# A hybrid decoder layer on one core: the input projections of both FFNs as seven block products

## The chip, the core and the metric

The kernel runs on one core of a Trainium2 chip. The core has TensorE (PE in the rows; its weight loads are PEld), VectorE (DVE), ScalarE (ACT), GpSimd (POOL) and SyncE (SP), which only issues transfers here. The metric is the device time of one execution in microseconds (us), and less is better.

## The reference, cut to what matters

One decoder layer on 512 tokens of width 1024, in float32: a half-step FFN, a token mixer, a second half-step FFN of the same shape, and a per-layer embedding. The change concerns the two FFNs:

```python
D_MODEL = 1024; SEQ = 512; D_FF = 2816

def swiglu(u, w_in, w_out):
    gate, up = jnp.split(u @ w_in, 2, axis=-1)
    return (jax.nn.silu(gate) * up) @ w_out

# step 1 and step 3 of the layer
h = h + 0.5 * rmsnorm(swiglu(rmsnorm(h, norm_pre), w_in, w_out), norm_post)
```

`u @ w_in` is the input projection: 512 tokens x 1024 by 1024 x 5632. `@ w_out` is the output projection, 2816 to 1024.

## The kernel before, in words

**Precision.** Every float32 matrix is held as two fp32r tiles, a rounded one (hi: `whi`, `uhi`) and the rest (lo: `wlo`, `ulo`). `mm3` makes one product of three matmuls: hi by hi, hi by lo, lo by hi (lines 100 to 102). ACT makes the hi tile by a cast, DVE the lo tile by a subtraction of two SBUF tiles: for a weight tile, line 91 is the cast and line 92 the subtraction.

**Input projection.** The 2816 hidden features are 22 tiles of 128, and a tile f has two weight chunks of 128 x 1024 (512 KB), gate and up. `wchunk` loads a chunk into one of two `raw` buffers over SP's queue and splits it into one of three `whi`/`wlo` pairs. In `ffn`, PE multiplies a chunk with all 512 tokens into one PSUM bank `pgu`: 8 parts of the 1024-deep sum by three matmuls of 512 columns, so 48 matmuls for a tile f. `ev` then takes the bank: ACT's Silu of the gate (line 259), DVE's product with the up part (262), and the split of the result into `hid[f]` (263 on ACT, 266 on DVE).

**Start of an FFN.** `make_u` normalises one tile of 128 tokens, PE transposes it into `put`, and ACT and DVE split it into `uhi` and `ulo`. Since tokens 0 to 255 come first, `start_tiles` runs the first chunks (6 in the first FFN, 4 in the second) in two halves of 256 columns; their bank is called `p` in the rows.

**After it.** `out_proj` multiplies `hid` with the output weights (bank `acc`), and norms and adds the result. Between the FFNs lies the mixer. Its rows serve below as examples: there GpSimd adds two SBUF tiles of 128 x 512 (line 983) while DVE splits weight tiles.

Each engine works through its instructions in one fixed order, which a scheduler chose from the program's order; an instruction that waits holds up all those behind it on its engine.

Of the kernel before, what the change touches and what calls it, by code (L numbers as in the profile page):

```python
# [32 lines left out]
def layer_kernel(ctx, tc, x, pT, wf1, wo1, wfm, wsm, wtm, wbr, wout, wf2, wo2, wgate, wproj,  # L33
# [82 lines left out]
    def u_at(u, k, n):  # L116
        return u[0][:, k, n], u[1][:, k, n]
# [10 lines left out]
    def first_u(tt, h, u, t):

        hs = sp.tile([128, 1], F32, name="hs", bufs=4)  # L130
        A.activation(t, h[:, tt, :], AF.Square, accum_out=hs)
        V.tensor_scalar(t, h[:, tt, :], inv_rms(hs, False), None, op0=ALU.mult)
        tk = slice(tt * 128, tt * 128 + 128)
        for j in range(2):
            pt = axp("put")
            for i in range(4):
                k = 4 * j + i
                tr(pt[:, i * 128:(i + 1) * 128], t[:, k * 128:(k + 1) * 128])
            for i in range(4):
                k = 4 * j + i  # L140
                g = cst[:, C_G + k:C_G + k + 1]
                pv = pt[:, i * 128:(i + 1) * 128]
                A.activation(u[0][:, k, tk], pv, AF.Copy, scale=g)
            for i in range(4):
                k = 4 * j + i
                g = cst[:, C_G + k:C_G + k + 1]
                pv = pt[:, i * 128:(i + 1) * 128]
                V.scalar_tensor_tensor(u[1][:, k, tk], pv, g, u[0][:, k, tk].bitcast(F32),
                                       op0=ALU.mult, op1=ALU.subtract)

    def make_u(tt, h, gn, u, t):
# [4 lines left out]
        V.scalar_tensor_tensor(t, h[:, tt, :], r, gn, op0=ALU.mult, op1=ALU.mult)  # L156
        tk = slice(tt * 128, tt * 128 + 128)
        for j in range(2):
            pt = axp("put")
            for i in range(4):  # L160
                k = 4 * j + i
                tr(pt[:, i * 128:(i + 1) * 128], t[:, k * 128:(k + 1) * 128])
            pv = pt.rearrange("p (a b) -> p a b", b=128)
            ks = slice(4 * j, 4 * j + 4)
            A.copy(u[0][:, ks, tk], pv)
            V.tensor_sub(u[1][:, ks, tk], pv, u[0][:, ks, tk].bitcast(F32))
# [53 lines left out]
                if ch:  # L220
                    close(tt, 1 + len(cut))

    def start_tiles(tiles, u):

        for si, n in enumerate(SEG):
            for i, (w, r, ev) in enumerate(tiles):
                ps = (mmp if si == 0 else axp)("p0")
                for k in range(KT):
                    mm3(ps[:r, n], cols(w, k * r, (k + 1) * r), u_at(u, k, n), k == 0, k == KT - 1)
                ev(n, ps)  # L230
# [7 lines left out]
    def start_weights(fp, wf, n, slots):  # L238
        for i in range(n):
            dst = None  # L240
            if i >= slots:
                c = 14 + 2 * (i - slots)
                dst = (fp.tile([128, 1024], F32R, name=f"xh{i}", tag=f"hid{c}"),
                       fp.tile([128, 1024], F32R, name=f"xl{i}", tag=f"hid{c + 1}"))
            yield wchunk(wf[i], dst=dst, eng=G if wf is wf2 and i > 1 else None)

    def ffn(fp, free, wf, wo, h, u, gi, gn_i, first):
        hid = [None] * FT
        marks = []
        g = {}  # L250

        def ev(f, part):
            def run(n, ps):
                if part == 0:
                    if f == 2 and len(first) == 6:
                        t = g[f] = lp.tile([128, T + 608], F32, name="gx")
                    else:
                        t = g[f] = sp.tile([128, T], F32, name="gt", tag="t512", bufs=2)
                    A.activation(t[:, n], ps[:, n], AF.Silu)
                else:  # L260
                    t = g[f]
                    V.tensor_tensor(t[:, n], ps[:, n], t[:, n], op=ALU.mult)  # L262
                    m = A.copy(hid[f][:, 0, n], t[:, n])
                    if f == 4:
                        marks.append(m)
                    V.tensor_sub(hid[f][:, 1, n], t[:, n], hid[f][:, 0, n].bitcast(F32))
            return run

        def hid_tile(f):
            return fp.tile([128, 2, T], F32R, name=f"hid{f}")  # L270

        nf = len(first) // 2
        for f in range(nf):
            hid[f] = hid_tile(f)
        start_tiles([(w, 128, ev(i // 2, i % 2)) for i, w in enumerate(first)], u)
        for f in range(nf, FT):
            hid[f] = hid_tile(f)
# [34 lines left out]
    with pool("s1", "right") as small:  # L312
        env.small = small
        f1_pool = ExitStack()
        fp = f1_pool.enter_context(pool("f1"))
        xt = [small.tile([128, D], F32, name=f"ys{i}") for i in range(2)]
# [5 lines left out]
        weights = start_weights(fp, wf1, 6, 2)  # L322
# [7 lines left out]
        u = new_u()  # L330
        for tt in range(4):
            if tt < 1:
                first_u(tt, h, u, xt[tt % 2])
            else:
                make_u(tt, h, gn, u, xt[tt % 2])
        u = ffn(fp, f1_pool.close, wf1, wo1, h, u, G_F1 + 1, G_MIX, first)
# [623 lines left out]
    if True:  # L960
# [27 lines left out]
        u2 = new_u()  # L988
# [132 lines left out]
```

## Time and profile before

| what | value |
|---|---|
| time, median of 3 runs | 1319.95 us (1317.66 to 1321.33) |
| time of the profiled execution | 1320.2 us |
| its span, first to last instruction | 1318.4 us |
| PE busy (98% of the span) | 1287.5 us |
| PEld busy | 1074.3 us |
| DVE busy | 639.3 us |
| ACT busy | 465.7 us |
| POOL busy | 70.0 us |
| bytes moved | 141.26 MB, 107 GB/s on average |

The profile is of one execution. The span is 1.8 us shorter than that execution's time. A matmul's busy time overlaps that of the next one, so the pace of PE is read from the distance of two starts, not from one duration. The first FFN's input projection lies at about 13 to 260 us of the span, the second one's at about 887 to 1130 us.

### The profile page before, as it was taken

To read this page: it belongs to the slowest core of one execution; us is meant where nothing else is said; L and a number is where in the kernel's file an instruction comes from. 1 tells how busy PE (TensorE), PEld (TensorE's weight loads), DVE (VectorE), ACT (ScalarE), POOL (GpSimd) and SP (SyncE) were. 2 spreads that over 40 slices of the span, in tenths; PEclk is the share of its full clock that TensorE was granted. 3 is DMA by queue.
4 is the path that set the end of the run, shared out by engine and by line. 5 is a ranking of instruction groups with operands and counts; after the bars stand their busy time and mean duration, and the time that the engine had idled before them with its cause. 6 is when DMAs were issued, how large, how long until landed. Compare 5 with 4: busy or idle time off the path is not lost.

```text
span 1318.4 us, 16647 instructions
## 1 busy us (share of the span) xinstructions
PE 1287.5 (98%) x6661; PEld 1074.3 (81%) x6661; DVE 639.3 (48%) x1088; ACT 465.7 (35%) x765; POOL 70.0 (5%) x71
## 2 busy tenths in 40 slices
PE   7999999999989999999999999989999999999997
PEld 6988888888879888877678888779888888888876
DVE  6233333323262699987686454463333333223465
ACT  6222222212253453454655222352222223112353
POOL 0000000000010000021002001220000000000000
PEclk9999999999999999999999999999999999999999
DMA  6243333223342223344206635522433333233431
GB/s 216 67 128 96 96 96 98 94 83 99 122 143 92 88 65 111 97 121 130 79 1 147 212 108 181 159 87 81 130 96 96 96 96 108 68 96 96 128 112 64
DMA packets 57772, 141.26 MB, mean 107 GB/s; under 512 B 17568, under 2 KB 20064, under 8 KB 57696
## 3 DMA queue, kind: packets, MB, share of 16 engines
q1 hardware_dynamic: 56688, 136.54, 33.9%
q10 hardware_dynamic: 1008, 3.67, 0.9%
q8 instruction: 52, 0.85, 0.3%
q14 instruction: 24, 0.20, 0.0%
HBM read 128.62 MB, written 11.57 MB: 106 GB/s over the span
## 4 chain that ended last, share of the span: by engine, by line
PE 86%; DMA 5%; DVE 5%; ACT 2%; issue 1%; POOL 0%; SPq 0%; DVEq 0%; POOLq 0%; ACTq 0%
PE pgu L101 11%; PE pgu L100 11%; PE pgu L102 11%; PE acc L101 5%; PE acc L102 5%; PE acc L100 5%; PE p L101 3%; PE p L100 3%; PE p L102 3%; PE ptm L101 2%; PE ptm L100 2%; PE ptm L102 2%; PE pg L100 2%; PE pg L102 2%; PE pg L101 2%; PE pat L713 2%
## 5 line engine op out<-in xcount | busy, mean ns | idle before, releaser
L91 ACT CAST whi<-raw 128x1024 fp32r<-128x1024 f32 x135 | 142.1, 1052 | 389.7 <-PE pgu L101 154.0
L92 DVE TENSOR_TENSOR wlo<-raw,whi 128x1024 fp32r<-128x1024 f32 x135 | 166.3, 1232 | 195.0 <-ACT whi L91 187.6
L100 PE MATMUL pgu<-uhi,whi 128*128 128x512 f32 x624 | 242.8, 389 | 0.0
L102 PE MATMUL pgu<-uhi,wlo 128*128 128x512 f32 x624 | 242.8, 389 | 0.0
L101 PE MATMUL pgu<-ulo,whi 128*128 128x512 f32 x624 | 242.7, 389 | 0.0
L100 PEld LDWEIGHTS pgu<-uhi,whi 128*128 128x128 f32 x624 | 117.1, 188 | 24.5
L102 PEld LDWEIGHTS pgu<-uhi,wlo 128*128 128x128 f32 x624 | 117.1, 188 | 24.4
L101 PEld LDWEIGHTS pgu<-ulo,whi 128*128 128x128 f32 x624 | 117.1, 188 | 24.0
L92 DVE TENSOR_TENSOR vlo<-raw,vhi 128x1024 fp32r<-128x1024 f32 x45 | 56.1, 1249 | 131.0 <-ACT vhi L91 130.9
L101 PE MATMUL acc<-vlo,hid 128*128 128x512 f32 x288 | 112.1, 389 | 0.0
L102 PE MATMUL acc<-vhi,hid 128*128 128x512 f32 x288 | 111.7, 389 | 0.0
L91 ACT CAST vhi<-raw 128x1024 fp32r<-128x1024 f32 x45 | 47.1, 1048 | 143.7 <-PE acc L102 123.3
L100 PE MATMUL acc<-vhi,hid 128*128 128x512 f32 x288 | 97.4, 389 | 0.0
L262 DVE TENSOR_TENSOR gt<-pgu,gt 128x512 f32<-128x512 f32 x39 | 27.0, 692 | 136.7 <-PE pgu L102 136.7
L78 POOL TENSOR_TENSOR rinv<-ms,mhalf 128x1 f32<-128x1 f32 x32 | 18.9, 594 | 844.0 <-DVE ms L123 844.0
L101 PEld LDWEIGHTS acc<-vlo,hid 128*128 128x128 f32 x288 | 54.1, 188 | 11.3
L100 PEld LDWEIGHTS acc<-vhi,hid 128*128 128x128 f32 x288 | 54.1, 188 | 11.2
L102 PEld LDWEIGHTS acc<-vhi,hid 128*128 128x128 f32 x288 | 54.0, 188 | 11.3
L101 PE MATMUL ptm<-wlo,uhi 128*128 128x512 f32 x128 | 50.3, 393 | 0.0
L100 PE MATMUL ptm<-whi,uhi 128*128 128x512 f32 x128 | 50.0, 395 | 0.0
L102 PE MATMUL ptm<-whi,ulo 128*128 128x512 f32 x128 | 49.8, 391 | 0.0
L100 PE MATMUL pg<-uhi,whi 128*128 128x512 f32 x104 | 41.2, 396 | 0.0
(394 smaller groups left out, 2335.9 us busy)
## 6 DMA issues: line engine op xcount, KB each, us to landing
raw<-wf SPq DMA_DIRECT2D x88, 512.0 KB, 3.6
raw<-wo SPq DMA_DIRECT2D x44, 512.0 KB, 3.6
raw<-wfm SPq DMA_DIRECT2D x28, 512.0 KB, 3.7
raw<-wtm SPq DMA_DIRECT2D x20, 512.0 KB, 3.7
gd<-gst SPq DMA_DIRECT2D x16, 256.0 KB, 2.1
raw<-wbr SPq DMA_DIRECT2D x8, 512.0 KB, 4.4
grl<-gd SPq DMA_DIRECT2D x16, 256.0 KB, 3.2
raw<-wout SPq DMA_DIRECT2D x8, 512.0 KB, 4.2
```

Source lines behind the costliest of these rows:

```text
L78: G.tensor_tensor(out_, in_, e, op=ALU.pow)
L91: A.copy(hi[:, :n], raw[:, :n])
L92: (eng or V).tensor_sub(lo[:, :n], raw[:, :n], hi[:, :n].bitcast(F32))
L100: PE.matmul(ps, l[0], r[0], start=start, stop=False)
L101: PE.matmul(ps, l[0], r[1], start=False, stop=False)
L102: PE.matmul(ps, l[1], r[0], start=False, stop=stop)
L262: V.tensor_tensor(t[:, n], ps[:, n], t[:, n], op=ALU.mult)
L713: PE.matmul(pa[:, :S], qbT[b:b + 64, pr, tt * 128:tt * 128 + 128], kbT[b:b + 64, pr, :S], start=True, stop=True)
```

## The change

Let the two halves of the 1024-deep sum be the rows of a 2 by 2 block matrix, gate and up chunk of one tile f its columns, and tokens 0 to 255 and 256 to 511 the two column blocks of the other factor. Before, the four blocks of the result took eight block products (of 128 features, a 512-deep sum and 256 tokens). Now they take seven, in Winograd's form of Strassen's scheme. A block product is 4 parts by three matmuls of 256 columns, 12 matmuls, so a tile f has 84.

What else there is for it:

- For each tile f, GpSimd makes four sums and differences of the two raw chunks, 128 x 512 each (`sa`, `sb`, lines 374 to 377). Four weight operands are then split into hi and lo: x1 (the raw gate chunk), x2 (`sa`), x3 (`sb`), 128 x 1024 each, and x4 (half of the raw up chunk), 128 x 512.
- The seven products are gathered in `ct` by DVE: one addition of a PSUM bank and an SBUF tile, 128 x 256, at a time (six at line 386, one at 353). ACT copies the product of x1 first (344) and makes Silu of either token half (354, 402). The gate-by-up product of tokens 0 to 255 is DVE's (399), that of tokens 256 to 511 is GpSimd's (403).
- `Ops` makes the token operands once for each FFN. `second_half` forms differences of the token halves on DVE and GpSimd and splits them into T1 (in `uhi`/`ulo`), T2, T3 and T4 (the tile `hz` of the residual, which is read back from DRAM before the output projection).
- The x1 products of the first four tiles (`NF`) need only tokens 0 to 255; they run first, around the transposes of the other tokens, and their gate chunks are loaded a second time in the main loop.
- Buffers: the raw chunks go round four slots (two `raw`, and two that hold `ys0`, `ys1` and `second_half`'s `ta`, `tb` before), the split weights round four pairs, `sa` and `sb` have one buffer each.

```diff
+        def second_half(self, tt, t, after):
...
+            V.tensor_tensor(ta[:, 0], p[0], b11, op=ALU.subtract)
+            V.tensor_tensor(ta[:, 1], p[1], ta[:, 0], op=ALU.subtract)
+            parts([x[:, :, b] for x in self.t2], ta[:, 1])
+            G.tensor_tensor(tb[:, 1], b21, ta[:, 1], op=ALU.subtract)
+            V.tensor_tensor(tb[:, 0], ta[:, 1], b11, op=ALU.subtract)
+            parts([x[:, :, b] for x in self.t3], tb[:, 0])
+            parts([x[:, 0:4, n] for x in self.u], ta[:, 0])
+            parts([x[:, :, b] for x in self.t4], tb[:, 1])
+            parts([x[:, 4:8, n] for x in self.u], p[1])
+            return last
...
-            for i in range(2):
-                w = wchunk(wf[2 * f + i])
-                ps = mmp("pgu")
-                for k in range(KT):
-                    mm3(ps, cols(w, k * 128, (k + 1) * 128), u_at(u, k, ALL), k == 0, k == KT - 1)
-                ev(f, i)(ALL, ps)
...
+        def product(w, c, b):
+            banks[0] += 1
+            ps = (mmp, axp)[banks[0] % 2]("pf")[:, N1]
+            for k in range(4):
+                m = mm3(ps, cols(w, c + k * 128, c + k * 128 + 128), o.at(b, k), k == 0, k == 3)
+            return m, ps
...
+        order = [(p1, 0), (p1, 1), (p2, 0), None, (p1, 2), (p2, 1), (p1, 3), None, (p2, 2), (p2, 3)]
...
+        for f in range(FT):
+            g, u_ = load_raw(wf[2 * f]), load_raw(wf[2 * f + 1])
...
+            G.tensor_tensor(sa[:, h1], u_[:, h1], u_[:, h2], op=ALU.add)
+            G.tensor_tensor(sa[:, h2], sa[:, h1], g[:, h1], op=ALU.subtract)
+            G.tensor_tensor(sb[:, h1], g[:, h1], u_[:, h1], op=ALU.subtract)
+            G.tensor_tensor(sb[:, h2], g[:, h2], sa[:, h2], op=ALU.subtract)
+            if f >= NF:
+                x1 = parts(ring(), g)
+            x2 = parts(early(fp, 2) if f == 0 else ring(), sa)
+            x3 = parts(early(fp, 3) if f == 0 else ring(), sb)
+            x4 = parts([o.hz[:, 2 + f % 2, h] for h in (h1, h2)], u_[:, h2])
+            if f >= NF:
+                p1(f, x1)
+            c = ct[f]
+            add = lambda dst, ps, a: V.tensor_tensor(dst, ps, a, op=ALU.add)
+            _, ps = product(x2, 512, "T2")
+            add(c[:, 1], ps, c[:, 0])
+            _, ps = product(x3, 0, "T3")
+            add(c[:, 2], ps, c[:, 1])
+            _, ps = product(x2, 0, "T1")
+            add(c[:, 3], ps, c[:, 2])
+            add(c[:, 1], ps, c[:, 1])
+            if f >= NF:
+                p2(f, x1)
+            t = ts.pop(f)
+            _, ps = product(x4, 0, "T4")
+            add(c[:, 2], ps, c[:, 2])
+            V.tensor_tensor(t[:, N1], t[:, N1], c[:, 2], op=ALU.mult)
+            _, ps = product(x3, 512, "B22")
+            add(c[:, 1], ps, c[:, 1])
+            A.activation(t[:, N2], c[:, 1], AF.Silu)
+            G.tensor_tensor(t[:, N2], t[:, N2], c[:, 3], op=ALU.mult)
+            hid[f] = fp.tile([128, 2, T], F32R, name=f"hid{f}")
+            parts([hid[f][:, 0], hid[f][:, 1]], t)
+
+        h = hp.tile([128, 4, D], F32, name="hr", tag="hz")
+        for tt in range(4):
+            SY.dma_start(h[:, tt, :], hsrc(tt))
```

The order on DVE before, in the middle of the first FFN's input projection: these five rows hold the four of one tile f (two weight subtractions, the product, the split of `hid`) and the first of the next.

```order
L92 TENSOR_TENSOR wlo<-raw,whi 128x1024
L262 TENSOR_TENSOR gt<-pgu,gt 128x512
L92 TENSOR_TENSOR wlo<-raw,whi 128x1024
L266 TENSOR_TENSOR hid_847<-gt,hid_847 128x512
L92 TENSOR_TENSOR wlo<-raw,whi 128x1024
```

The order on DVE of the changed kernel at the same place, one tile f (`ct_1062` is f = 6). The first row gathers T2 and T3 of this tile; x2 and x3 (`wlo<-sa`, `wlo<-sb`) are those of f = 7, x4 (`t_209`) and x1 (`wlo<-raw`) those of f = 8, and `hid_1035` is that of f = 5.

```order
L386 TENSOR_TENSOR ct_1062<-pf,ct_1062 128x256 x2
L329 TENSOR_TENSOR hid_1035<-gt,hid_1035 128x512
L386 TENSOR_TENSOR ct_1062<-pf,ct_1062 128x256 x2
L329 TENSOR_TENSOR wlo<-sa,whi 128x1024
L353 TENSOR_TENSOR gt<-pf,ct_1062 128x256
L329 TENSOR_TENSOR wlo<-sb,whi 128x1024
L386 TENSOR_TENSOR ct_1062<-pf,ct_1062 128x256
L329 TENSOR_TENSOR t_209<-raw,t_209 128x512
L386 TENSOR_TENSOR ct_1062<-pf,ct_1062 128x256
L399 TENSOR_TENSOR gt<-gt,ct_1062 128x256
L329 TENSOR_TENSOR wlo<-raw,whi 128x1024
L386 TENSOR_TENSOR ct_1194<-pf,ct_1194 128x256 x2
```

Where DVE had four instructions for a tile f, it has thirteen now, and the subtractions that PE's next tile needs stand between additions that wait for this tile's products.

GpSimd had nothing in the input projections but the reciprocal roots of the norms: the first rows of before go from the roots of the first norms straight to those of the mixer, with its copies and masks.

```order
L78 TENSOR_TENSOR rinv<-ms,mhalf 128x1 x12
L78 TENSOR_TENSOR rki<-kss,mhalf 128x4
L511 COPY ki<-ki 128x4x64
L558 AFFINE_SELECT sc_3148<-sc_3148 128x128
L558 AFFINE_SELECT sc_3200<-sc_3200 128x128
```

GpSimd of the changed kernel while DVE goes through the rows above: the product of f = 5, the four sums of f = 8 (they need `sa` and `sb` free of f = 7), the product of f = 6 and the first sum of f = 9.

```order
L403 TENSOR_TENSOR gt<-gt,ct_930 128x256
L374 TENSOR_TENSOR sa<-raw 128x512
L375 TENSOR_TENSOR sa<-sa,raw 128x512
L376 TENSOR_TENSOR sb<-raw 128x512
L377 TENSOR_TENSOR sb<-raw,sa 128x512
L403 TENSOR_TENSOR gt<-gt,ct_1062 128x256
L376 TENSOR_TENSOR sb<-rawy 128x512
```

So each tile f brings GpSimd five instructions that read two SBUF operands, two tiles ahead of PE.

## Rows read from the trace of the kernel before

**Rows 1.** The page, busy time of the whole span.
```profile
PE 1287.5 (98%) x6661; PEld 1074.3 (81%) x6661; DVE 639.3 (48%) x1088; ACT 465.7 (35%) x765; POOL 70.0 (5%) x71
```

**Rows 2.** Windows: busy us (x count) of PE, PEld, DVE, ACT, POOL; PEclk, DMA share, GB/s.
```profile
53.00:259.90 206.90, 206.90 (x915) 171.32 (x914) 69.38 (x75) 58.58 (x75) 0.00 (x0) 1.00 0.32 100
912.50:1130.00 217.50, 217.50 (x963) 180.09 (x962) 73.13 (x79) 61.83 (x79) 0.00 (x0) 1.00 0.33 100
12.60:53.00 40.40, 39.56 (x305) 39.27 (x306) 20.54 (x31) 17.90 (x29) 1.10 (x2) 1.00 0.42 124
886.60:912.50 25.90, 25.90 (x203) 25.86 (x203) 11.37 (x17) 8.48 (x16) 3.95 (x4) 0.92 0.33 102
```

**Rows 3.** Timeline of PE (start, us, instruction), 512-column matmuls of pgu.
```profile
100.16 0.39 PE L101 MATMUL pgu<-ulo,whi 128*128 128x512 f32 x1
...
100.84 0.39 PE L101 MATMUL pgu<-ulo,whi 128*128 128x512 f32 x1
```

**Rows 4.** Timeline of PE, 256-column matmuls of p.
```profile
30.09 0.28 PE L101 MATMUL p<-ulo,xh 128*128 128x256 f32 x1
...
33.33 0.28 PE L101 MATMUL p<-ulo,xh 128*128 128x256 f32 x1
```

**Rows 5.** Groups of DVE by line and form (busy us, mean ns | idle).
```profile
L92 DVE TENSOR_TENSOR wlo<-raw,whi 128x1024 fp32r<-128x1024 f32 x135 | 166.3, 1232 | 195.0 <-ACT whi L91 187.6 <-PE pg L102 1.8
...
L266 DVE TENSOR_TENSOR hid<-gt,hid 128x512 fp32r<-128x512 f32 x39 | 26.7, 685 | 1.4 <-ACT hid L263 1.4
...
L262 DVE TENSOR_TENSOR gt<-p,gt 128x256 f32<-128x256 f32 x8 | 3.4, 422 | 9.0 <-PE p L102 9.0
```

**Rows 6.** Groups of ACT by line and form.
```profile
L91 ACT CAST whi<-raw 128x1024 fp32r<-128x1024 f32 x135 | 142.1, 1052 | 389.7 <-PE pgu L101 154.0 <-issue 124.8 <-PE pc L101 35.6
...
L263 ACT CAST hid<-gt 128x512 fp32r<-128x512 f32 x39 | 24.2, 621 | 11.2 <-DVE gt L262 11.2
```

**Rows 7.** Group of POOL by line and form, a 512-column add.
```profile
L983 POOL TENSOR_TENSOR grl<-grl,ybm 128x512 f32<-128x512 f32 x8 | 12.8, 1617 | 26.6 <-DVE grl L982 22.9 <-ACT vhi L91 3.7
```

**Rows 8.** Timeline of POOL, the same add in four places of the mixer.
```profile
814.34 1.29 POOL L983 TENSOR_TENSOR grl<-grl,ybm 128x512 f32<-128x512 f32 x1 [12.28 <-DVE grl L982]
816.83 1.67 POOL L983 TENSOR_TENSOR grl<-grl,ybm 128x512 f32<-128x512 f32 x1 [1.20 <-DVE grl L982]
822.19 2.31 POOL L983 TENSOR_TENSOR grl<-grl,ybm 128x512 f32<-128x512 f32 x1 [3.70 <-ACT vhi L91]
```

**Rows 9.** Timeline of DVE at those places.
```profile
817.27 2.31 DVE L92 TENSOR_TENSOR vlo<-raw,vhi 128x1024 fp32r<-128x1024 f32 x1
...
822.13 1.23 DVE L92 TENSOR_TENSOR vlo<-raw,vhi 128x1024 fp32r<-128x1024 f32 x1
...
885.34 1.29 DVE L166 TENSOR_TENSOR ulo<-put,uhi 128x512 fp32r<-128x512 f32 x2 [0.35 <-ACT uhi L165]
```

**Rows 10.** Timeline of POOL, two 1024-column subtractions before the second FFN.
```profile
883.95 5.54 POOL L92 TENSOR_TENSOR xl<-raw,xh 128x1024 fp32r<-128x1024 f32 x2 [0.70 <-ACT xh L91]
```

**Rows 11.** Timeline of PE after a wait (in brackets: idle time, releaser).
```profile
592.52 0.47 PE L100 MATMUL pc<-uhi,whi 128*128 128x512 f32 x1 [2.47 <-ACT DT L650]
...
594.24 0.63 PE L100 MATMUL pc<-uhi,whi 128*128 128x512 f32 x1
594.67 0.63 PE L101 MATMUL pc<-ulo,whi 128*128 128x512 f32 x1
```

**Rows 12.** Timeline of ACT, first FFN, cast of the fourth weight tile.
```profile
20.63 1.05 ACT L91 CAST xh<-raw 128x1024 fp32r<-128x1024 f32 x1 [0.91 <-DMA raw<-wf]
```

**Rows 13.** Timeline of DVE, last normalised token tile before the second FFN.
```profile
894.01 1.29 DVE L156 SCALAR_TENSOR_TENSOR ys<-h,rinv,gn 128x1024 f32<-128x1024 f32 x1 [0.73 <-POOL rinv L78]
```

**Rows 14.** Timeline of PE, first matmuls of the output projections.
```profile
259.74 0.39 PE L100 MATMUL acc<-vhi,hid 128*128 128x512 f32 x1
```

More of the change, by code (lines that the diff above doesn't have):

```diff
@@ L101, in mm3 @@
         PE.matmul(ps, l[0], r[1], start=False, stop=False)
-        PE.matmul(ps, l[1], r[0], start=False, stop=stop)
+        return PE.matmul(ps, l[1], r[0], start=False, stop=stop)
     def cols(pair, a, b):
@@ L126, in inv_rms, with normed @@
         return r
[L128 to L151, printed above, removed]
+    def normed(tt, h, t, gn=None):
         hs = sp.tile([128, 1], F32, name="hs", bufs=4)
@@ L157, in make_u @@
+    def make_u(tt, h, gn, u, t):
+        normed(tt, h, t, gn)
         tk = slice(tt * 128, tt * 128 + 128)
@@ L236, in sandwich_tail @@
         return finish
[L238 to L277, printed above, removed]
-            for i in range(2):
-                w = wchunk(wf[2 * f + i])
-                ps = mmp("pgu")
-                for k in range(KT):
-                    mm3(ps, cols(w, k * 128, (k + 1) * 128), u_at(u, k, ALL), k == 0, k == KT - 1)
-                ev(f, i)(ALL, ps)
@@ new lines, in sandwich_ops, with finish, early, start_weights @@
+    def sandwich_ops(h, ys, gn, o):
+        def finish(tt, r):
+            V.scalar_tensor_tensor(h[:, tt, :], ys[tt], r, h[:, tt, :], op0=ALU.mult, op1=ALU.add)
+            SY.dma_start(hdram[:, tt, :], h[:, tt, :])
+            normed(tt, h, ys[tt], gn)
+            if tt < 2:
+                o.first_half(tt, ys[tt])
+        return finish
+    NF = 4
+    def early(fp, i):
+        return [fp.tile([128, 1024], F32R, name=f"xh{i}{k}", tag=f"hid{14 + 2 * i + k}") for k in range(2)]
+    def start_weights(fp, wf):
+        for f in range(NF):
+            yield wchunk(wf[2 * f], dst=early(fp, 0) if f == 3 else None)
@@ new lines, in ffn, with ring, load_raw, parts @@
+    def ffn(fp, free, wf, wo, hsrc, o, ys, first, gi, gn_i):
+        small = env.small
+        hid, ct = [None] * FT, {}
+        count = [0, 0]
+        N1, N2 = SEG
+        def ring():
+            n = count[0]
+            count[0] += 1
+            if n % 4 == 3:
+                return [small.tile([128, 1024], F32R, name=f"xr{k}", tag=f"ys{2 + k}") for k in range(2)]
+            return [wp.tile([128, 1024], F32R, name=nm, tag=nm, bufs=3) for nm in ("whi", "wlo")]
+        def load_raw(src):
+            n = count[1] % 4
+            count[1] += 1
+            t = (wp.tile([128, 1024], F32, name="raw", tag="raw", bufs=2) if n < 2 else
+                 small.tile([128, 1024], F32, name="rawy", tag=f"ys{n - 2}"))
+            SY.dma_start(t, src)
+            return t
+        def parts(dst, src):
+            A.copy(dst[0], src)
+            V.tensor_sub(dst[1], src, dst[0].bitcast(F32))
+            return dst
+        banks = [0]
+        def product(w, c, b):
[4 more added lines that the diff above has]
+            return m, ps
+        def p1(f, w):
+            ct[f] = fp.tile([128, 4, 256], F32, name=f"ct{f}", tag=f"hid{f}")
+            m, ps = product(w, 0, "B11")
+            A.copy(ct[f][:, 0], ps)
+            return m
+        ts = {}
+        def p2(f, w):
+            m, ps = product(w, 512, "B21")
+            t = ts[f] = sp.tile([128, T], F32, name="gt", tag="t512", bufs=2) if f >= NF else fp.tile(
+                [128, T], F32, name=f"gf{f}", tag=f"hid{10 + f}")
+            V.tensor_tensor(t[:, N1], ps, ct[f][:, 0], op=ALU.add)
+            A.activation(t[:, N1], t[:, N1], AF.Silu)
+            return m
+        order = [(p1, 0), (p1, 1), (p2, 0), None, (p1, 2), (p2, 1), (p1, 3), None, (p2, 2), (p2, 3)]
+        last, tt = None, 2
+        for step in order:
+            if step is None:
+                last = o.second_half(tt, ys[tt], last)
+                tt += 1
+            else:
+                with (tc.issue_after(last.ins) if last is not None else ExitStack()):
+                    last = step[0](step[1], first[step[1]])
+        for f in range(FT):
+            g, u_ = load_raw(wf[2 * f]), load_raw(wf[2 * f + 1])
+            if f == 0:
+                sa, sb = [t.bitcast(F32) for t in early(fp, 1)]
+            else:
+                sa = small.tile([128, 1024], F32, name="sa", tag="gp")
+                sb = small.tile([128, 1024], F32, name="sb", tag="gn")
+            h1, h2 = slice(0, 512), slice(512, 1024)
+            G.tensor_tensor(sa[:, h1], u_[:, h1], u_[:, h2], op=ALU.add)
[33 more added lines that the diff above has]
+            SY.dma_start(h[:, tt, :], hsrc(tt))
@@ L285, in ffn @@
         gp = env.small.tile([128, D], F32, name="gp")
         gn = env.small.tile([128, D], F32, name="gn")
-        with tc.issue_after(marks[0].ins):
-            A.dma_start(gp, gain_row(gi))
-            A.dma_start(gn, gain_row(gn_i))
+        SY.dma_start(gp, gain_row(gi))
+        SY.dma_start(gn, gain_row(gn_i))
         ys = [env.small.tile([128, D], F32, name=f"ys{tt}") for tt in range(4)]
@@ L293, in load @@
         def load(ch, j, a):
+            dst = None
             if a is None:
-                dst = upper(fp)
+                if ch or j > 1:
+                    dst = upper(fp)
             else:
@@ L302, in ffn @@
                  ys, gp, sandwich_tail(h, ys, gn, u2), free)
-        return u2
+        return h, u2
     hdram = dp.tile([128, 4, D], F32, name="hdram")
@@ L315, in layer_kernel @@
         fp = f1_pool.enter_context(pool("f1"))
-        xt = [small.tile([128, D], F32, name=f"ys{i}") for i in range(2)]
+        ys = [small.tile([128, D], F32, name=f"ys{i}") for i in range(4)]
         SY.dma_start(h[:, 0, :], x[0])
@@ L321, in layer_kernel @@
         SY.dma_start(gn, gain_row(G_F1))
-        weights = start_weights(fp, wf1, 6, 2)
+        weights = start_weights(fp, wf1)
         first = [next(weights)]
@@ L329, in layer_kernel @@
         SY.dma_start(prm, params)
-        u = new_u()
+        o = Ops()
         for tt in range(4):
[L332 to L336, printed above, removed]
+            normed(tt, h, ys[tt], gn if tt else None)
+            if tt < 2:
+                o.first_half(tt, ys[tt], tt == 0)
+        o.open(fp)
+        h, u = ffn(fp, f1_pool.close, wf1, wo1, lambda tt: x[tt], o, ys, first, G_F1 + 1, G_MIX)
         for tt in range(4):
```

72 lines of the change are left out of this document (60 added, 12 removed).

## The prediction

> **What bounds the kernel now.** I read the page first: PE is busy for 98% of the span [rows 1]. Then the windows of the two input projections: PE is busy without a gap at the full granted clock, DVE and ACT for a third of the time, GpSimd for none, the transfers for a third [rows 2]. So PE's pace is the time of these stages, and the others have room. The pace is the distance of starts: three 512-column matmuls take 0.68 us, so 0.2267 us each [rows 3], and a tile f of 48 takes 10.88 us. The timeline also has 256-column matmuls, whose 27 steps from 30.09 to 33.33 us are 0.120 us each [rows 4]: a little more than half of 0.2267.
>
> **The change, part by part.**
>
> *PE.* A tile f takes 84 matmuls of 256 columns, 84 x 0.120 = 10.08 us, in place of 10.88. That is 0.80 us less, not an eighth (1.36), since halving the columns costs 6%. This is the floor of the new loop, and the whole prize is 44 x 0.80 = 35 us, a little more with the first ten chunks, which ran in halves already.
>
> *DVE's own work* for a tile f, by the rows of like shape [rows 5]: three 1024-column subtractions (1.23 each, 3.69), two of 512 (0.685, 1.37), seven additions from PSUM and one product, 256 columns each (0.42, 3.38). Together 8.4 us of 10.08, where it was 2 x 1.23 + 0.69 + 0.69 = 3.8 of 10.88.
>
> *ACT* casts 3 x 1.05 + 2 x 0.62 [rows 6] and makes three passes over 256 columns, at most 0.62 each: 6.3 us. It has room, so I cost it at nothing except where it stands in a chain.
>
> *GpSimd* makes four sums of 512 columns and a product of 256. Undisturbed, such an add takes 1.29 us (the first of rows 8); the group's mean is 1617 ns [rows 7]. So 4 x 1.29 and some 0.7 for the product, 5.9 us. This alone would fit.
>
> *GpSimd beside DVE* does not. At 816.83 us GpSimd begins an add of two SBUF tiles and ends it at 818.50. DVE's subtraction of two SBUF tiles begins at 817.27 and takes 2.31 us in place of 1.23: it ends 1.08 us after GpSimd's end. At 822.13 the turn is the other way: DVE ends at 823.36, and GpSimd's add, begun at 822.19, takes 2.31 in place of 1.29, ending 1.14 us after DVE's end [rows 8, 9]. The one waits for the other's whole instruction. But four DVE subtractions that read one operand from PSUM, beginning at 885.34, keep their usual time (two in 1.29 us) under GpSimd's long subtractions [rows 9, 10]. So what excludes each other are instructions with two SBUF operands.
> The Trainium skill (SBUF — State Buffer, "Who interferes with whom") says the same more generally: the port pair that VectorE and GpSimd share is an exclusive lock, the second to come is blocked until the first ends, and a VectorE instruction with two SBUF inputs takes part in it. By it the sums on GpSimd are not free work on an idle engine; if the two shared bandwidth in place of taking turns, rival 1's time would follow. These rows agree with the lock (1.08 and 1.14 us left after the other's end).
>
> *The sum of turns* for a tile f: GpSimd 4 x 1.14 + 0.6 = 5.2; DVE's six instructions with two SBUF operands, 3 x 1.08, 2 x 0.55 and 0.3, 4.7. Together 9.9 us of PE's 10.08: nothing is left for a turn that comes at the wrong moment. And DVE works in order, with additions that do not need a turn between those that do.
>
> *A walk through one tile f*, by the printed orders and these durations. Time 0 is the end of x2's subtraction, which sets `sa` free, so GpSimd's sums of the tile after next start exactly now. Sum 1 runs to 1.3. DVE adds (0.4), then x3's subtraction waits for 1.3 and ends at 2.4. Sum 2 runs to 3.55. DVE adds, x4's subtraction waits and ends at 4.1. Sum 3 to 5.25; DVE adds, and its product waits and ends at 5.55. Sum 4 to 6.7; x1's subtraction waits and ends at 7.8. GpSimd's product runs to 8.4, DVE adds twice to 8.65; ACT casts `hid` (0.62) to 9.05, DVE subtracts it to 9.75, adds twice to 10.6, and the next tile's first heavy subtraction ends at 11.8. Nothing in this round waited for PE: the products come each 1.44 us and are ready before their additions. So DVE, at 8.4 us of its own and 3.4 of waiting, sets the pace: **11.8 us for a tile f**, 0.9 more than before. Bounds: below, 10.08 (every turn falls into a gap); above, 8.4 + 5.2 = 13.6 (DVE waits out all of GpSimd's turns). I take the walk.
>
> *The start of an FFN.* First FFN: PE begins its products as before, near 13 to 14 us. The fourth weight tile is cast at 20.63 us [rows 12], after three that follow at about 3 us each; the two raw chunks of f = 0 use the same two buffers next, so they land near 23.5 and 26.5. GpSimd's sums, a cast and a subtraction each bring x2 and x3 to 30 to 33. DVE has more: from 23 us on, two `second_half` of eight 512-column instructions (5.5 us each), four additions (1.7), x2, x3, x4 (3.1) and the turns with GpSimd. The first product of T2 can start near 36 and f = 0 ends near 45; PE, whose eight first products (11.5 us) and 16 transposes are done near 29, waits some 7 us. The chunks of f = 1 land in `ta` and `tb` after these are read, near 43: two sums (2.6), a cast, a subtraction, so T2 at 49.5 and its end at 57. The tiles f = 2 and 3 have five products (7.2) and a turn sum of 8; I take 8, so the main loop stands at 73 us after four tiles. The other 18 take 18 x 11.8 = 212: the stage ends at 285 us, where the output projection now starts at 259.7 [rows 14]: **+26 us**.
> Second FFN: the weights and chunks of f = 0 are there early. The last token tile is normalised at 894 + 1.3 [rows 13], then its transposes, its `second_half` and the rest of the same DVE list: T2 near 903, f = 0 done at 911, f = 1 at 922, f = 3 at 938, and with 212 the end is at 1150, where it is 1130 now (the end of the second window in [rows 2]): **+20 us**.
>
> *What is moved or added beside it.* Each FFN loads four chunks twice (2 MB) and the residual again (2 MB). The transfers are busy for 0.32 of these stages [rows 2], so they hide; if they did not, 4 MB at the 100 GB/s of [rows 2] would be 40 us spread over 270. SP issues the residual's four loads after the last T4 product and ahead of later output weights; the first two of these are issued before. The first output weights use the split pairs of the loop. For both hand-overs I take +2 us together (0 to 8: at the upper end one wait of a load in each). The transposes and norms of the other stages stay as they are.
>
> The sum: 1318.4 + 26 + 20 + 2 = 1366 us of span, and with the 1.8 us around it **1368 us** against 1320.2 of the profiled execution (the median, 1319.95, is the same within 0.02%).
>
> **The rivals.**
>
> 1. *Faster: the turns fall into gaps.* The scheduler set the orders so that each subtraction is due some microseconds ahead, and 9.9 us of turns are less than 10.08. Then PE paces: 73 + 18 x 10.08 = 254.4 and 938 + 181.4 = 1119.4, so -5 and -11, +2: 1306 us. It decides where a tile f takes under 10.5 us, the mean of (259.7 - 73)/18 = 10.4 and (1130 - 938)/18 = 10.7. Against it: in the walk nearly every turn collides, since one event starts GpSimd's sums and DVE's densest stretch.
> The Trainium skill (TensorE: Matmul & The Clock Gate, "Back-to-back issue gap") gives columns/2.4 + 2.5 ns for the distance of warm matmuls, 109 ns here; by it this rival would come out some 33 us lower still (36 x 84 x 0.011). The row has 120 ns for these shapes with their weight loads, and the row decides.
> 2. *In between:* GpSimd, whose sums also wait for single-buffered `sa` and `sb`, spreads out, and DVE catches up where PE holds it. 10.5 to 11.2 us a tile, 1321 to 1346 us.
> 3. *Slower still: the clock falls.* PE waits about 1.7 us in each tile. After a wait of 2.47 us the 512-column matmuls go at 0.43 us, the lower level of 1.2 GHz, for eight of them [rows 11]: 8 x 0.2 = 1.6 us lost. If each of 36 tiles paid that and DVE's lag did not cover it, 58 us more, near 1425. For it: the waits are of that size. Against it: in the walk PE's results are ready 2 to 3 us before DVE takes them, which covers 1.6.
>
> **How the numbers follow.** The forecast, 11.2 to 12.6 us a tile (36 x 0.6 below to 36 x 0.8 above, 1346 to 1397), has 0.64; rival 1 0.13; rival 2 0.12; rival 3, or turns near their upper bound, 0.11. The likeliest is 1368. The range leaves out most of rivals 1 and 3: 1318 to 1402. A measurement of this kernel can tell 0.3%, 4 us, from no change. Faster has rival 1 but for its upper edge, 0.12; same takes that edge and the lower edge of rival 2, 0.05; slower 0.83.
>
> **What the profile of the changed kernel would show.** Right: in the main loop PE's product tile has idle time, ended by DVE (`wlo` or `xr` at line 329); DVE is the busiest with GpSimd near 7 us a tile; the mean of DVE's 1024-column subtractions is 1.7 us or more in place of 1.23, that of GpSimd's sums 1.5 or more in place of 1.29, while the additions from PSUM keep 0.42. Tiles follow each other in 11.8 us, and the stages end near 285 and 1175 (1150 shifted by the first 26). Wrong: PE without gaps at 0.120 us and subtractions of 1.23; then rival 1. The clock row of the loop well under 1 with waits of PE for itself would speak for rival 3. What would make the prediction wrong most easily is the walk's start: if GpSimd's sums began at another point of DVE's round, fewer turns would collide.

## The result, and the profile after

The changed kernel took 1378.67 us (median of 4 runs, 1377.50 to 1380.17), the one before 1318.87 beside it: a ratio of 1.045, 95% interval 1.043 to 1.047. The forecast was 1368, in a range of 1318 to 1402: slower, as forecast, 10.7 us more than its number. That it came so near is in part luck: steps of the sum were off in opposite directions; they are named below. One of the four executions of E8 below took 1423.08 us at a lower granted clock (0.943, the others 0.972 to 0.975) and is left out of its time.

The page of the changed kernel: busy time, then the span in 40 slices of tenths.

```profile
span 1378.4 us, 20522 instructions
...
PE 1283.3 (93%) x8005; PEld 1128.7 (82%) x8005; DVE 974.5 (71%) x1494; ACT 563.4 (41%) x951; POOL 418.8 (30%) x293
...
PE   6688989899999999999999999987989899999997
...
DVE  6799999952254689986685454667999999623465
...
PEclk9899999999999999999999999998999999999999
```

PE's share fell from 98% [rows 1] to 93%; in the slices of the two input projections (2 to 7 and 28 to 33, counted from 0) DVE stands at 9 throughout and PE falls to 8 in half of them. The windows of these stages (their columns as in [rows 2]):

```profile
45.00:75.00 30.00, 23.64 (x175) 22.93 (x174) 20.99 (x26) 11.18 (x15) 24.55 (x16) 0.89 0.36 123
75.00:265.00 190.00, 171.91 (x1369) 166.84 (x1370) 184.96 (x216) 82.11 (x128) 129.53 (x84) 0.98 0.26 90
910.00:940.00 30.00, 22.00 (x141) 20.61 (x138) 23.92 (x33) 16.85 (x32) 10.54 (x10) 0.83 0.24 88
940.00:1180.00 240.00, 213.48 (x1667) 207.03 (x1666) 224.75 (x266) 102.97 (x159) 164.30 (x105) 0.96 0.27 93
```

Where PE had been busy for all 206.9 us of the first stage [rows 2], it is busy for 171.9 of 190; VectorE went from a third to 97%, GpSimd from nothing to 68%, and the transfers' share stayed at 0.26, so they are not what holds the loop up. The groups of lines over the whole program, with the mean of one instruction in ns and PE's idle time with what ended it:

```profile
L102 PE MATMUL pf<-vhi,wlo 128*128 128x256 f32 x248 | 77.9, 314 | 24.2 <-DVE wlo L329 24.2
...
L329 DVE TENSOR_TENSOR wlo<-sb,whi 128x1024 fp32r<-128x1024 f32 x30 | 57.0, 1902 | 1.0 <-ACT whi L328 1.0
...
L329 DVE TENSOR_TENSOR wlo<-sa,whi 128x1024 fp32r<-128x1024 f32 x32 | 49.4, 1545 | 4.9 <-ACT whi L328 4.9
...
L375 POOL TENSOR_TENSOR sa<-sa,rawy 128x512 f32<-128x512 f32 x22 | 41.1, 1867 | 1.6
...
L329 DVE TENSOR_TENSOR wlo<-raw,whi 128x1024 fp32r<-128x1024 f32 x18 | 36.0, 2001 | 0.0
...
L353 DVE TENSOR_TENSOR gt<-pf,ct 128x256 f32<-128x256 f32 x36 | 15.0, 416 | 0.0
```

The signs that the prediction named are there: PE waits for `wlo` (24.2 us in this group alone), the 1024-column subtractions average 1.55 to 2.00 us in place of 1.23, GpSimd's second sum 1.87 (all four 1.67) in place of 1.29, and the additions that read PSUM keep 0.42. One tile f of the main loop on VectorE:

```profile
152.17 1.22 DVE L329 TENSOR_TENSOR wlo<-sa,whi 128x1024 fp32r<-128x1024 f32 x1
153.30 0.42 DVE L353 TENSOR_TENSOR gt<-pf,ct 128x256 f32<-128x256 f32 x1
153.64 2.26 DVE L329 TENSOR_TENSOR wlo<-sb,whi 128x1024 fp32r<-128x1024 f32 x1
...
156.15 1.44 DVE L329 TENSOR_TENSOR t<-rawy,t 128x512 fp32r<-128x512 f32 x1
...
157.85 1.18 DVE L399 TENSOR_TENSOR gt<-gt,ct 128x256 f32<-128x256 f32 x1
158.95 2.31 DVE L329 TENSOR_TENSOR xr<-rawy,xr 128x1024 fp32r<-128x1024 f32 x1
...
162.54 0.69 DVE L329 TENSOR_TENSOR hid<-gt,hid 128x512 fp32r<-128x512 f32 x1 [0.42 <-ACT hid L328]
...
163.82 1.21 DVE L329 TENSOR_TENSOR wlo<-sa,whi 128x1024 fp32r<-128x1024 f32 x1
```

and GpSimd beside it:

```profile
153.52 1.30 POOL L374 TENSOR_TENSOR sa<-rawy 128x512 f32<-128x512 f32 x1 [3.01 <-issue]
154.89 2.15 POOL L375 TENSOR_TENSOR sa<-sa,rawy 128x512 f32<-128x512 f32 x1
157.00 1.74 POOL L376 TENSOR_TENSOR sb<-rawy 128x512 f32<-128x512 f32 x1
158.71 1.47 POOL L377 TENSOR_TENSOR sb<-rawy,sa 128x512 f32<-128x512 f32 x1
160.14 1.72 POOL L403 TENSOR_TENSOR gt<-gt,ct 128x256 f32<-128x256 f32 x1
```

Two starts of x2's subtraction, 152.17 and 163.82, are 11.65 us apart. GpSimd's sums begin at 153.52, just behind that subtraction. The next four heavy instructions of VectorE (153.64, 156.15, 157.85, 158.95) take 2.26, 1.44, 1.18 and 2.31 us, where 1.22, 0.68, 0.41 and 1.21 would do: 3.7 us of waiting, for a turn each. Their ends show the turns: each lies 1.08, 0.55, 0.29 and 1.08 us behind the end of the GpSimd instruction beside it (the first: 153.52 + 1.30 = 154.82, and 153.64 + 2.26 = 155.90), which are the prediction's times for a turn. VectorE's idle time in this tile is only the 0.42 us at 162.54.

The stages' ends, by PE's first matmul of each: output projection of the first FFN (259.74 before [rows 14]), input projection of the second, output projection of the second.

```profile
291.67 0.39 PE L100 MATMUL acc<-whi,hid 128*128 128x512 f32 x1
```
```profile
917.19 0.39 PE L100 MATMUL pf<-uhi,whi 128*128 128x256 f32 x1 [2.42 <-ACT uhi L176]
```
```profile
1190.90 0.39 PE L100 MATMUL acc<-whi,hid 128*128 128x512 f32 x1
```

The first stage ends 31.9 us later. The second FFN's took 1130.0 - 886.7 = 243.3 us [rows 2] and takes 273.7, 30.4 more. The rest of the program is 2.3 us shorter (60.0 - 31.9 - 30.4).

### The profile page after: what moved, and what is told of

Same layout as the page of the kernel before. It is cut to its first block, busy times and chain, and to the rows that moved or that the text cites. A ratio compares the mean times of both kernels' runs of the same rounds, so it can differ in the third digit from the quotient of the medians.

```text
span 1378.4 us, 20522 instructions
## 1 busy us (share of the span) xinstructions
PE 1283.3 (93%) x8005; PEld 1128.7 (82%) x8005; DVE 974.5 (71%) x1494; ACT 563.4 (41%) x951; POOL 418.8 (30%) x293
## 3 DMA queue, kind: packets, MB, share of 16 engines
q1 hardware_dynamic: 60144, 149.12, 31.9%
## 5 line engine op out<-in xcount | busy, mean ns | idle before, releaser
L100 PE MATMUL pf<-uhi,whi 128*128 128x256 f32 x520 | 151.4, 291 | 6.8 <-ACT uhi L176 3.4
L101 PE MATMUL pf<-ulo,whi 128*128 128x256 f32 x520 | 151.1, 291 | 3.6 <-DVE ulo L177 3.6
L102 PE MATMUL pf<-uhi,wlo 128*128 128x256 f32 x520 | 150.9, 290 | 1.2 <-DVE wlo L92 1.2
L92 DVE TENSOR_TENSOR wlo<-raw,whi 128x1024 fp32r<-128x1024 f32 x65 | 80.7, 1241 | 56.3 <-ACT whi L91 52.7
L91 ACT CAST whi<-raw 128x1024 fp32r<-128x1024 f32 x65 | 68.3, 1051 | 111.9 <-PE pc L101 35.6
L100 PEld LDWEIGHTS pf<-uhi,whi 128*128 128x128 f32 x520 | 102.9, 198 | 7.8 <-ACT uhi L176 4.0
L386 DVE TENSOR_TENSOR ct<-pf,ct 128x256 f32<-128x256 f32 x264 | 104.9, 413 | 5.9 <-PE pf L102 1.4
L101 PEld LDWEIGHTS pf<-ulo,whi 128*128 128x128 f32 x520 | 103.1, 198 | 4.1 <-DVE ulo L177 4.1
L102 PEld LDWEIGHTS pf<-uhi,wlo 128*128 128x128 f32 x520 | 103.0, 198 | 1.5 <-DVE wlo L92 1.5
L102 PE MATMUL pf<-vhi,wlo 128*128 128x256 f32 x248 | 77.9, 314 | 24.2 <-DVE wlo L329 24.2
```

The costliest lines, as they stand in the source:

```text
L91: A.copy(hi[:, :n], raw[:, :n])
L92: (eng or V).tensor_sub(lo[:, :n], raw[:, :n], hi[:, :n].bitcast(F32))
L102: return PE.matmul(ps, l[1], r[0], start=False, stop=stop)
L386: add = lambda dst, ps, a: V.tensor_tensor(dst, ps, a, op=ALU.add)
```

## The experiments

Each kernel is the changed one with the edit shown. A tile's pace is the mean distance of the starts of the gate-by-up product (line 399 of the changed kernel) in the middle of the loop; the changed kernel repeats 11.38, 11.68, 11.88, 11.56, mean 11.62 us.

**E1, no sums.** The four `G.tensor_tensor` lines go, and:

```diff
-            x2 = parts(... ring(), sa)
-            x3 = parts(... ring(), sb)
+            x2 = parts(... ring(), g)
+            x3 = parts(... ring(), u_)
```

> GpSimd's four sums of a tile f are left out; x2 and x3 are split from the raw gate and up chunk, so the products are of other weights. GpSimd keeps only its 256-column product. Theory (VectorE's own 8.4 us plus its waits for GpSimd's turns set the pace): the waits go, 8.4 is under 10.08, PE paces the main loop at 10.08 us in place of 11.62 us a tile, the 1024-column subtractions go back to 1.23 us; 16 tiles x 1.54 = 25 us less in each FFN, and some 8 us less in each start: about 1313 us (1300 to 1325). Rival (VectorE's fixed order with PE's results between is the pace, whoever makes the sums): over 11 us a tile, over 1350 us.

Measured: 1292.35 us, ratio to before 0.979 (0.977 to 0.981). The windows of the changed kernel and of E1 over the same stretch of the first loop:

```profile
100.00:240.00 140.00, 127.81 (x1015) 124.17 (x1014) 136.21 (x158) 62.04 (x98) 94.36 (x61) 0.98 0.26 91
```

```profile
100.00:240.00 140.00, 140.00 (x1188) 140.00 (x1187) 109.05 (x184) 76.05 (x114) 19.82 (x15) 1.00 0.31 102
```

PE has no gap any more, 9.93 us a tile (0.118 us a matmul), and VectorE 31 us of room in 140. So without the sums PE paces, as the theory said; the time is 21 us under the forecast and below its range, because the start of each FFN became shorter by more than the 8 us that I had given it; of the 43.6 us that the first FFN gains here, the loop makes 27 (16 x 1.69). All of the sums, wherever they act, cost 86.3 us: 43.6 in the first FFN (291.67 - 248.12, the end of that stage in E1) and 43.7 in the second.

**E2, sums that nobody reads.** As E1, but GpSimd's four lines stay.

> GpSimd makes its four sums as before, but nothing reads them: x2 and x3 are split from the raw chunks as in the run without sums. Theory (the turns on the port): 11.0 to 11.6 us a tile, subtractions of 1024 columns well over 1.23 us, 1355 to 1379 us. Rival (what costs is the chain from a sum over cast and subtraction to the product, or the single buffers of sa and sb, which nobody waits for here): PE paces at 10.08, near 1313 us as without sums.

Measured: 1340.8 us, ratio 1.015 (1.013 to 1.017); 10.7 us a tile.

```profile
100.00:240.00 140.00, 132.80 (x1108) 131.47 (x1108) 128.86 (x170) 67.99 (x106) 116.45 (x67) 1.00 0.28 99
```

Sums on which nothing waits cost 48.5 us over E1. The rival is out: more than half of what the sums cost is not their chain to the product. The theory's lower end, 1355, was too high, though: 0.9 us a tile of the changed kernel is missing here. The groups of lines over the same stretch, of which this is one, show where it lies:

```profile
L329 DVE TENSOR_TENSOR wlo<-raw,whi 128x1024 fp32r<-128x1024 f32 x17 | 26.9, 1582 | 0.0
```

Added up, the subtractions and products of lines 329 and 399 are 32 us longer than undisturbed in these 140 us, 2.4 us a tile; in the changed kernel it is 47.5 us, 3.9 a tile. VectorE's idle time rose, from 0.3 to 0.9 us a tile. So what is missing is waiting for turns, not waiting for a sum. E8 and E9 ask whether the moment of the sums decides it.

**E3, the sums on VectorE.** `V.tensor_tensor` in place of `G.tensor_tensor` in the four lines.

> The four sums are VectorE's in place of GpSimd's, with the same operands and results. Theory: VectorE has 8.4 + 4 x 0.685 = 11.1 us of its own and hardly a wait for a turn (one product of 256 columns on GpSimd, 0 to 0.6): 11.1 to 11.7 us a tile, GpSimd idle, subtractions at 1.23; 1362 to 1382 us, so about the same time from another cause. Rival (GpSimd's slower sums, 1.29 to 1.9 against 0.685, are what PE waits for): under 10.6 us a tile, below 1345 us.

Measured: 1311.0 us, ratio 0.993 (0.991 to 0.995): 0.7% faster than before, and 51 us under the theory's range.

```profile
100.00:240.00 140.00, 139.93 (x1180) 139.73 (x1179) 139.06 (x240) 72.86 (x114) 25.59 (x14) 1.00 0.31 107
```

The expectation failed, and its sum with it: VectorE does all that work, 240 instructions in 140 us, and PE has hardly a gap; the pace is about 10.1 us a tile. VectorE cannot have 11.1 us of its own. The rival's number came out, but not for its reason, since sums that no one waits for already cost time (E2), and VectorE in the changed kernel is idle for only 3.8 us of these 140. The mistake is in how I read durations; E7 shows it best.

**E4, other buffers.** The raw chunks of f = 1 go where those of f = 0 were:

```diff
-            n = count[1] % 4
+            n = count[1] % 4 if count[1] < 2 else (count[1] - 2) % 4
```

> Only the buffers of the raw chunks change: those of f = 1 go into the two raw buffers that f = 0 had (free at 35 us) and those of f = 2 into the two that held ta and tb (free at 45 us), where it was the other way. Theory (f = 1 waits for its chunks, which land at 48 us): they land near 39, the start of each FFN is up to 8 us shorter, the main loop stays at 11.6: 1362 us (1360 to 1370). Rival (in the start too the sums and VectorE set the pace): 0 to 3 us less in each FFN, 1373 to 1379 us.

Measured: 1370.74 us, ratio 1.038 (1.036 to 1.040), 7.9 us less than the changed kernel; the loop stays at 11.65. The first stage ends at 286.03, 5.6 us earlier, the second is 1.7 us shorter. The late load was real, and smaller than the up to 8 us of each FFN that I took it for.

**E5, both.** E3 and E4 together.

> The sums on VectorE and the other order of the raw buffers, together. Theory (with the sums on VectorE it has 9.70 us of its own for a tile by the distances of its starts, a little under PE's 9.93, and is without a gap from 47 us on; before that it waits 3.2 us for the chunks of f = 1): the wait goes, 3 to 4 us less in each FFN, 1304 us (1301 to 1308), main loop unchanged at 10.1. Rival (VectorE's backlog of the start only moves, the wait was free): 1309 to 1313 us.

Measured: 1306.47 us (1302.60 to 1308.69), ratio 0.989 (0.987 to 0.991). In the range that was expected; with E7 the best version here that computes the layer, and faster than both kernels. The two stages of its profile are 3.9 and 0.7 us shorter than E3's, where the theory had 3 to 4 us in each: the second part of it did not show.

**E6, one sum back on GpSimd.** E5 with `G.tensor_tensor` for `sb[:, h2]`.

> As the run before it, but the last of the four sums is GpSimd's again. Theory (turns): VectorE's own work falls to 9.10 us, and a turn of 1.14 us on GpSimd returns, which is free only where it falls on additions from PSUM; about half of it collides, so 9.9 to 10.3 us a tile and 1300 to 1310 us, no clear difference to the run before. Rival (less work on VectorE is what counts): PE paces at 9.93 and the start is shorter, below 1298 us.

Measured: 1309.4 us, ratio 0.992 (0.990 to 0.993). No clear difference to E5, as expected: 0.6 us of work less on VectorE bought nothing.

**E7, nothing on GpSimd.** E5 with the product of line 403 on VectorE.

> As e5, and the product of tokens 256 to 511 is VectorE's too, so GpSimd does nothing in the loop. Theory: VectorE 9.70 + 0.34 = 10.04 us of its own and no turn to wait for: every subtraction at 1.21 and sum at 0.68, 10.05 us a tile, 1301 to 1307 us, equal to e5 within 4 us. Rival (the product on GpSimd is a free 0.34 us): 0.3 a tile slower, 1314 us or more.

Measured: 1306.04 us, ratio 0.989 (0.987 to 0.991); 10.0 us a tile. VectorE's timeline there, with no gap and no turn to wait for:

```profile
154.14 0.70 DVE L375 TENSOR_TENSOR sa<-sa,rawy 128x512 f32<-128x512 f32 x1
154.75 0.43 DVE L399 TENSOR_TENSOR gt<-gt,ct 128x256 f32<-128x256 f32 x1
155.08 0.43 DVE L353 TENSOR_TENSOR gt<-pf,ct 128x256 f32<-128x256 f32 x1
...
156.68 1.23 DVE L329 TENSOR_TENSOR xr<-sa,xr 128x1024 fp32r<-128x1024 f32 x1
157.82 0.76 DVE L386 TENSOR_TENSOR ct<-pf,ct 128x256 f32<-128x256 f32 x2
```

Look at distances, not at durations. A 512-column sum of 0.70 us is followed after 0.61 (154.14, 154.75), a 256-column product of 0.43 after 0.33 (154.75, 155.08), a 1024-column subtraction of 1.23 after 1.14 (156.68, 157.82). Each instruction's duration overlaps the next one's by some 0.09 us.

**E8, two buffers for `sa`.**

```diff
-                sa = small.tile([128, 1024], F32, name="sa", tag="gp")
+                sa = (lp.tile([128, T + 608], F32, name="gx")[:, 0:1024] if f % 2 else
+                      small.tile([128, 1024], F32, name="sa", tag="gp"))
```

> The changed kernel with its sums on GpSimd, but sa alternates between two buffers, so GpSimd's first two sums need not begin at the end of x2's subtraction. All work stays. Theory (VectorE is busy all the time and only the moment of GpSimd's turns changes, as where nobody read the sums): between 10.7 and 11.6 us a tile, 1345 to 1372 us. Rival (the moment does not matter, each sum costs VectorE its turn wherever it begins): 11.6 us a tile, 1376 to 1381 us.

Measured: 1378.03 us, ratio 1.044 (1.041 to 1.046); 11.5 us a tile. The number is the rival's, but the edit didn't do what it was for. VectorE's x2 subtraction and GpSimd's first sum in E8:

```profile
153.72 1.22 DVE L329 TENSOR_TENSOR wlo<-sa,whi 128x1024 fp32r<-128x1024 f32 x1
```
```profile
155.02 1.32 POOL L375 TENSOR_TENSOR sa<-raw 128x512 f32<-128x512 f32 x1 [2.96 <-DVE wlo L329]
```

The sum still begins right at the end of an x2 subtraction (153.72 + 1.22 = 154.94): GpSimd only works a tile further ahead, into the buffer just released. The moment did not change, so the run tells nothing about it.

**E9, the sums behind the product.** E8, and:

```diff
+            with (tc.issue_after(muls[f - 2].ins) if f - 2 in muls else ExitStack()):
                 G.tensor_tensor(sa[:, h1], ...)   # the four sums
...
-            G.tensor_tensor(t[:, N2], t[:, N2], c[:, 3], op=ALU.mult)
+            muls[f] = G.tensor_tensor(t[:, N2], t[:, N2], c[:, 3], op=ALU.mult)
```

> The changed kernel with its sums on GpSimd and the two buffers for sa; new is only the place of the four sums in GpSimd's list: behind its product of the tile two before, where it has that product behind the sums. (With two buffers alone the sums kept beginning 0.2 us after an x2 subtraction, so that run left the question open.) All work and every result stay. Theory (VectorE is never idle for long, what differs is how many of its instructions meet a turn of GpSimd): the sums meet other instructions, as where nobody read them, 10.5 to 11.2 us a tile and 1340 to 1368 us. Rival (what slows the changed kernel beyond the run with unread sums is the wait of x2 and x3 for their sums): 11.5 us a tile or more, 1374 us or more.

Measured: 1359.05 us, ratio 1.028 (1.025 to 1.030); 10.9 us a tile. The number is the theory's: the same work and the same results in another order are 0.6 us a tile cheaper than E8, 0.7 than the changed kernel. More than GpSimd's moment moved, though: its four sums come in another order, and so does VectorE's list (the addition of line 353 stands in front of x2's subtraction here, not behind it, and additions and at times the product come between x2's and x3's). The run does not separate these. GpSimd's product and first sum, what VectorE then waits for, and the window of the loop:

```profile
157.49 1.54 POOL L405 TENSOR_TENSOR gt<-gt,ct 128x256 f32<-128x256 f32 x1 [2.88 <-ACT gt L404]
158.99 2.26 POOL L376 TENSOR_TENSOR gx<-rawy 128x512 f32<-128x512 f32 x1
```

```profile
165.33 1.33 DVE L329 TENSOR_TENSOR wlo<-gx,whi 128x1024 fp32r<-128x1024 f32 x1 [1.54 <-ACT whi L328]
```

```profile
100.00:240.00 140.00, 133.39 (x1085) 129.59 (x1084) 114.77 (x170) 63.84 (x102) 97.77 (x64) 1.00 0.28 95
```

VectorE is busy for 114.8 us of 140 here and waits for ACT's cast of a sum that now comes late (1.54 us at 165.33). Counted as in E2, turns cost it 1.4 us a tile (3.9 in the changed kernel and in E8), and it is idle for 2.1. So fewer turns collide, and the chain from sum to product, which hardly showed in the changed kernel, begins to.

## Why the prediction held, step by step

**PE's pace.** Right: 84 x 0.120 was to be 10.08; E1 has 9.93.

**GpSimd and VectorE take turns.** Right, and shown by E1 to E3: with the sums away PE paces, with sums nobody reads 0.8 us a tile return, with the sums on VectorE nearly all of the wait is gone. The Trainium skill (SBUF — State Buffer, "Who interferes with whom") had said so of VectorE instructions with two SBUF inputs, and these runs agree: 48.5 us from unread sums, and 0.42 us, as ever, for the additions that read PSUM. Rival 1, PE pacing, is what comes where GpSimd leaves the port alone; no run with the four sums on GpSimd came near it. Rival 2's pace, 10.5 to 11.2 us a tile, is that of E2 and E9, where fewer turns collide; two buffers for `sa` alone (E8) did not bring it.

**VectorE's own 8.4 us.** Wrong, the first step that failed. I added durations. By the distances of starts (three of 1.13, two of 0.605, eight of 0.335) it is 3.39 + 1.21 + 2.68 = 7.28 us. The rows of before had it: two 512-column subtractions in 1.29 us [rows 9], not 2 x 0.685. I read PE by distances for this very reason, and VectorE not. The Trainium skill (Perfetto Trace Analysis, "Optimizing Scalar/DVE Operations") says that part of a profiled latency overlaps the next instruction; E7's 0.09 us agrees. With the four sums at 0.605 VectorE has 9.70 us, under PE's 9.93, which is why E3 is faster than before where I forecast the time of the changed kernel.

**Its 3.4 us of waiting.** Too low by about as much: 11.62 - 7.28 = 4.3 us. By the groups of lines from 100 to 240 us the subtractions and products at line 329 and 399 are 47.5 us longer than undisturbed and VectorE is idle for 3.8; over 12.05 tiles (140/11.62) that is 4.3 as well. The walk had the four colliding instructions and the wait for ACT's cast right, but gave the turns 3.0 us where the tile above has 3.7, and `hid` none (in that stretch its subtraction takes 1.07 us in the mean, 0.685 undisturbed). So 11.8 for a tile against 11.62 measured is two errors of about 1 us that cancel, which is luck.

**The start of an FFN.** Wrong, the second step that failed, and the larger one. I had the main loop at 73 us after four tiles, 9 us behind the kernel before. By the matmuls of the timeline up to 100 us, the changed kernel had done 456/84 = 5.4 tiles and the one before 3 + 208/48 = 7.3 (its first 288 are three tiles in halves): 1.9 tiles, 20.7 us at 10.88. The remaining 16.6 tiles at 0.69 us more make 11.4 us, where I had 16.6 for 18 tiles; the last two of the loop take only 9 us each (GpSimd's last sum of this FFN ends near 278 us; that this is the reason was not tried). So +32 is 20.7 + 11.4, not 9 + 17. VectorE and GpSimd in that start:

```profile
26.76 0.68 DVE L197 TENSOR_TENSOR ulo<-ta,uhi 128x512 fp32r<-128x512 f32 x1
27.36 1.78 DVE L203 TENSOR_TENSOR tb<-ta,gx 128x512 f32<-128x512 f32 x1
29.06 1.77 DVE L197 TENSOR_TENSOR vlo<-ta,vhi 128x512 fp32r<-128x512 f32 x1
...
54.45 2.15 DVE L329 TENSOR_TENSOR wlo<-sa,whi 128x1024 fp32r<-128x1024 f32 x1 [1.09 <-ACT whi L328]
```

```profile
26.99 1.60 POOL L202 TENSOR_TENSOR tb<-gx,ta 128x512 f32<-128x512 f32 x1 [6.81 <-DVE ta L200]
28.55 1.73 POOL L374 TENSOR_TENSOR xh<-raw 128x512 f32<-128x512 f32 x1
...
48.19 1.30 POOL L374 TENSOR_TENSOR sa<-rawy 128x512 f32<-128x512 f32 x1 [8.47 <-DMA rawy<-wf]
```

and PE after it:

```profile
54.47 0.38 PE L100 MATMUL pf<-vhi,whi 128*128 128x256 f32 x1 [4.70 <-ACT whi L328]
...
57.03 0.41 PE L100 MATMUL pf<-vhi,whi 128*128 128x256 f32 x1
57.25 0.41 PE L101 MATMUL pf<-vlo,whi 128*128 128x256 f32 x1
```

`second_half`'s subtractions meet its own difference on GpSimd (1.78 us at 27.36, beside 26.99) and the sums of f = 0 (1.77 at 29.06, beside 28.55; undisturbed such a one takes 0.68, as at 26.76), the chunk of f = 1 lands at 48.2 us behind `ta` and `tb` and not near 43, and T2 of f = 1 begins at 54.5 where I had 49.5. That the sums make the start, too, is shown by E1, where 7.1 tiles are done at 100 us, a quarter of a tile behind before; E4 gives the late chunk 5.6 us of it. E2, in which nothing waits for a sum, has done 472 matmuls there, 5.6 tiles: of the 139 that the changed kernel has less than E1, 123 are missing in E2 too. So most of the start's loss is not the chain of sum, cast and subtraction. How it divides between the turns and the raw chunks, which unread sums hold as long, was tried no further than E4.

**The second FFN** was to lose 20 us, less than the first, as its weights are there early. It lost 30.4, by the same kind of start: 86 us after its first product it is 1.8 tiles behind the kernel before (by matmuls, 5.7 against 7.5). The early weights did not help.

**The hand-overs** (+2 us, 0 to 8): all that lies outside the two stages, the hand-overs in it, is 2.3 us shorter. No loss shows; what the hand-overs take by themselves was not separated.

**Rival 3, the clock.** Not at a price in the loop. Its granted clock is 0.98 and 0.96, and 14 of PE's 20 waits from 75 to 265 us are under a microsecond. After one of the three longest, of 1.98 us, it did fall:

```profile
132.81 0.38 PE L102 MATMUL pf<-vhi,xr 128*128 128x256 f32 x1 [1.98 <-DVE xr L329]
...
133.45 0.41 PE L100 MATMUL pf<-vhi,xr 128*128 128x256 f32 x1
133.67 0.41 PE L101 MATMUL pf<-vlo,xr 128*128 128x256 f32 x1
```

The matmuls are 0.21 us apart there, the lower level of 1.2 GHz, for 3.4 us (and again from 225.5 us). The two tiles around it follow in 11.88 and 11.54 us, like those at the same place of the next four (11.89, 11.55), so VectorE's lag covered it, as the prediction's argument against this rival had it. In the starts it fell for longer: after the wait of 4.70 us the matmuls are at 0.21 us (57.03, 57.25) to 61.5 us, and then at 0.12 again. The windows have 0.89 and 0.83 there; I had costed this at nothing outside the rival.

## What to carry to other kernels

Add up an in-order engine's work from the distances of starts where it runs without a gap; a sum of durations overstated VectorE by 15% here and would have thrown away the version that wins. An engine that shows as idle is no free place for work that has to take turns with a neighbour's: four sums that cost VectorE 2.4 us a tile when it makes them leave it with 4.3 us of waiting when GpSimd does. Price the first tiles of a pipelined loop with the same care as its steady pace: two thirds of the first FFN's loss lay before 100 us, when the loop had hardly begun.

## What the runs showed of the hardware that was not expected

Back-to-back VectorE instructions of two tensors start 0.33, 0.605 and 1.13 us apart for 256, 512 and 1024 columns, some 0.09 us less than each shows as its duration in E7 (0.43, 0.70, 1.23). And the same instructions in another order on GpSimd and VectorE, with all work unchanged, moved the pace of the loop from 11.5 us (E8) to 10.9 (E9).
